# A transformer block with four mixers on one core: SBUF addresses of weight tiles, large tiles and constants, moved to 128 or 384 modulo 512

## The chip, the cores and the metric

The kernel runs on one core of one Trainium2 chip. The metric is the device time of one execution in microseconds (us). A profile of one execution was taken as well; it gives each instruction's engine, start and duration. Its engines are PE (TensorE: matmuls), PEld (TensorE's weight loads, which run beside the matmuls), DVE (VectorE), ACT (ScalarE), POOL (GpSimd) and SP (which issues DMAs).

## The reference

One block on `x` (512 tokens, width 1024): a normalised projection into four mixers of width 512 each, the mixers, an output projection with residual, and a last normalisation. All data is float32.

```python
def reference(x, mem, norm_g, w_in, ..., w_mem_kv, w_out, final_norm_g):
    for l in range(DEPTH):                                    # DEPTH = 1
        h = _rmsnorm(x, norm_g[l])
        p_fox, p_ssm, p_nsa, p_mem = _split(h @ w_in[l], [FOX_COLS, SSM_COLS, NSA_COLS, MEM_COLS])
        mem_kv = _rmsnorm(mem, mem_norm_g[l]) @ w_mem_kv[l]
        o = jnp.concatenate([
            _fox_mixer(p_fox, fox_f_bias[l]),                 # causal attention with forget gates
            _ssd_mixer(p_ssm, ...),                           # convolution and chunked state space scan
            _nsa_mixer(p_nsa, ..., rel_bias_table),           # compressed, selected and window attention
            _mem_mixer(p_mem, mem_kv),                        # attention to 256 memory tokens
        ], axis=-1)
        x = x + o @ w_out[l]
    return _rmsnorm(x, final_norm_g)
```

## The kernel before

**Number format.** Every large float32 product is done as three float32r matmuls (`three`, line 716): each operand is split into a high part and a low part, and high·high, high·low and low·high are summed in one PSUM bank. A matmul has a stationary operand of 128 x 128, loaded by a weight load (LDWEIGHTS) of its own, and a moving operand of up to 512 columns that streams past it.

**Weights.** All weights come as 75 tiles of 128 x 1024 in the order of `ORDER`. `load` brings a tile into a ring of three `raw` tiles; `split` makes its high part `wh` on ACT and its low part `wl = raw - wh` on POOL or DVE, in rings of three each (`ring`, line 568). The last eight tiles (output projection of the fourth mixer, `wo3`) are an exception: `split` puts their halves into tiles of 512 columns of the large pool `g`, by the names `lh` and `ll` (lines 605 to 609).

**Projections.** `tile_a` (line 873; PSUM tile `pj`) makes one 128 x 512 tile of a projection with 24 matmuls: stationary is a 128-column slice of `wh` or `wl`, moving are the parts `hh` and `hl` of the normalised input (512 columns, pool `g`). `proj_b` (line 762; `pb`), `mem_v` (line 1845; `pmv`) and the output projections `out_proj` and `out_last` (lines 1056 and 1086; `po`) have it the other way round: stationary is a 128-column slice of an activation (`uh`, `ul`; `mh`, `ml`; `oh`, `ol`), moving are 512 columns of `wh` or `wl` (in `out_last`, of `lh` or `ll`).

**Order.** The tile framework schedules nothing. The program's order is that of the code, with the steps of the mixers and of the projections interleaved by the written-out list `PLAN`. Each engine runs its instructions in that order and waits on semaphores.

**Where tiles lie.** Pool `g` has 58 places of 2048 bytes per partition (tiles of 512 float32 columns or less), pool `b` 12 places of 4096 bytes or a little more (`B4`, line 541), pool `sb` all rings and constants (`C1`, line 546), one after the other in the order in which the code asks for them. So a place's address follows from the sizes before it. By the tile allocation of the built program, the start addresses within a partition are, modulo 512:

| tiles | before | after |
|---|---|---|
| pool `g`, all 58 places (`hh`, `hl`, `uh`, `ul`, `oh`, `ol`, `lh`, `ll`, `mh` and the rest) | 128 | 128 |
| ring `raw` (3) | 128 | 384 |
| rings `wh`, `wl` (3 + 3) | 0 | 384 |
| pool `b`, 12 places (`xn`, `mt`, `ml`, `M`, `Rl`, `kh`, `kl`, `bt`, `acc` and the rest) | 128, 128, 256, 256, 256, 384, 0, 0, 0, 128, 256, 256 | 128, 128, 384, 384, 384, 128, 384, 384, 384, 128, 384, 384 |
| constants `ones`, `nv`, `w2`, `vcm`, `umask` | 256, 384, 384, 384, 128 | 128 each |
| constants `cst`, `x0` | 128, 128 | 384, 128 |

A 128-column slice of float32 is 512 bytes, so every stationary slice of a tile starts at the tile's own residue; so do the 512-column halves. The narrow projection `("bc", 0..2)` has slices of 296 columns (1184 bytes), which start at 0, 160 and 320 from the tile's start modulo 512.

Of the kernel before, what the change touches and what calls it, by code (L numbers as in the profile page):

```python
# [10 lines left out]
FT = mybir.dt.float32  # L11
# [19 lines left out]
RAW, RING = 3, 3  # L31
# [484 lines left out]
        return 0 < self.at[0] and self.at[-1] < len(self.steps)  # L516


@with_exitstack
def block_kernel(ctx, tc, I, out, lives):  # L520
    nc = tc.nc
# [1 line left out]
    V, A, P, T, Q = (Engine(e, n, clock, lives) for e, n in (  # L523
        (nc.vector, "DVE"), (nc.scalar, "ACT"), (nc.gpsimd, "POOL"), (nc.tensor, "PE"), (nc.sync, "SP")))
    NG, NB = 58, 12
    gp, bp, sp_, sb = (ctx.enter_context(tc.tile_pool(name=n, bufs=1)) for n in ("g", "b", "s", "sb"))
    ps = ctx.enter_context(tc.tile_pool(name="ps", bufs=1, space=bass.MemoryType.PSUM))
    dr = ctx.enter_context(tc.tile_pool(name="dr", bufs=1, space=bass.MemoryType.DRAM))
    ctx.enter_context(tc.manual_schedule())
# [2 lines left out]
    gslots, bslots = Slots("g", NG, lives, clock), Slots("b4", NB, lives, clock)  # L532
# [3 lines left out]
    def G(name, dt=FT, w=512, p=128):  # L536
        gs.take()
        tag, n = gslots.take()
        return gslots.hold(gp.tile([p, w], dt, name=name, tag=tag, bufs=n))

    def B4(name, shape, dt=FT):
        bs.take()
        tag, n = bslots.take()
        return bslots.hold(bp.tile(shape, dt, name=name, tag=tag, bufs=n))

    def C1(name, shape, dt=FT):
        n = math.prod(shape[1:])
        t = sb.tile([shape[0], -(-n // 32) * 32], dt, name=name)[:, :n]
        return t if len(shape) == 2 else t.rearrange("p (a b) -> p a b", a=shape[1])

    def SM(name, w):
        tag, n = sslots.take()
        return sslots.hold(sp_.tile([128, 64], FT, name=name, tag=tag, bufs=n))[:, :w]
# [5 lines left out]
    def PS(name):  # L559
        tag, n = pslots.take()  # L560
        t = pslots.hold(ps.tile([128, 512], FT, name=name, tag=tag, bufs=n))
        clock.bank(t.name)
        return t

    raw, wh, wl, state = {}, {}, {}, {"load": 0, "split": 0, "next": 0}
    rings = {"raw": [RAW, []], "wh": [RING, []], "wl": [RING, []]}

    def ring(name, dt):
        left = rings[name]
        t = sb.tile([128, 1024], dt, name=name, bufs={"raw": RAW, "wh": RING, "wl": RING}[name])  # L570
        assert left[0] > 0, "ring is full"
        left[0] -= 1
        if left[1]:
            clock.born[t.name] = left[1].pop(0)
        return t
# [7 lines left out]
    def load(n, wait=True):  # L583
        while state["load"] < min(n, len(ORDER)):
            i = state["load"]
            free = rings["raw"][1]
            if not wait and free and free[0] + SLACK > clock.t["PE"]:
                return
            raw[i] = ring("raw", FT)
            if i < 2:  # L590
                for h in range(2):
                    (A if i == h == 0 else Q).dma_start(out=raw[i][:, h * 512:(h + 1) * 512],
                                                        in_=I["wst"][i, :, h * 512:(h + 1) * 512])
                    if i == h == 0:
                        A.dma_start(out=x0[:, 264:520], in_=I["x0"][:, 264:520])
            else:
                Q.dma_start(out=raw[i], in_=I["wst"][i])
            state["load"] += 1

    def split(n):  # L600
        while state["split"] < min(n, len(ORDER)):
            i = state["split"]
            load(i + 1)
            halves = slice(0, 512), slice(512, 1024)
            if ORDER[i][0] == f"wo{LAST}":
                hi, lo = [G("lh", FR) for _ in halves], [G("ll", FR) for _ in halves]
                for x, h in enumerate(halves):
                    A.activation(hi[x], raw[i][:, h], AF.Copy)
                    tt(WIDE, out=lo[x], in0=raw[i][:, h], in1=hi[x].bitcast(FT), op=OP.subtract)
            else:  # L610
                hi, lo = ring("wh", FR), ring("wl", FR)
                for x, h in enumerate(halves if i < 2 else (slice(0, 1024),)):
                    if i == x == 0:
                        V.tensor_copy(out=hi[:, h], in_=raw[i][:, h])
                        low()
                    else:
                        A.activation(hi[:, h], raw[i][:, h], AF.Copy)
                    if i == x == 0:
                        V.tensor_tensor(out=lo[:, h], in0=raw[i][:, h], in1=hi.bitcast(FT)[:, h], op=OP.subtract)
                    else:  # L620
                        tt(WIDE, out=lo[:, h], in0=raw[i][:, h], in1=hi.bitcast(FT)[:, h], op=OP.subtract)
            wh[i], wl[i] = hi, lo
            unring("raw", raw.pop(i))
            state["split"] += 1
# [26 lines left out]
    def ahead():  # L651
        n = state["next"]
        load(min(n + 4, state["split"] + RAW), False)
        while can_split():
            split(state["split"] + 1)
            load(min(n + 4, state["split"] + RAW), False)

    x0 = C1("x0", [128, 632])
    vec = x0[:, 512:632]
    Q.dma_start(out=x0[:, 0:264], in_=I["x0"][:, 0:264])  # L660
    xt = [x0[:, 8:520]] + [G(f"xt{k}") for k in range(1, KT)]
    load(1)
    for k in range(1, KT):
        Q.dma_start(out=xt[k], in_=I["xT"][:, k, :])
        if k in (2, 5):
            load({2: 2, 5: 3}[k])
    xn = [B4("xn", [128, D]) for t in range(4)]
    for t in range(4):
        Q.dma_start(out=xn[t], in_=I["xn"][t])
    cst = C1("cst", [128, 788])  # L670
    Q.dma_start(out=cst, in_=I["cst"])
    Q.dma_start(out=x0[:, 520:632], in_=I["x0"][:, 520:632])
    ident, U, cmask, ind = cst[:, 0:128], cst[:, 128:256], cst[:, 256:768], cst[:, 768:776]
# [4 lines left out]
    v_pe = vec[:, 64:96]  # L678
    v_fd, v_al = vec[:, 96:112], vec[:, 112:120]

    ones = C1("ones", [128, 128])
    V.memset(ones, 1.0)
    nhalf = C1("nhalf", [128, 8])
    V.memset(nhalf, -0.5)

    seen = {}
# [41 lines left out]
    s4f = G("s4")  # L728
    P.memset(s4f, 0.0)
    fv = [G(f"fv{t}") for t in range(4)]  # L730
    nv = C1("nv", [128, 4, 296])
    uh, ul, hh, hl = [], [], [], []

    def parts(k):
# [9 lines left out]
    for k in range(KT):  # L744
# [4 lines left out]
            low()  # L749
        if k in (0, 3):  # L750
            split(1 if k == 0 else 2)
    rx = C1("rx", [128, 4])

    ss = SM("ss", 4)

# [65 lines left out]
    for i in range(2):  # L821
        t = B4("mt", [128, D])
        Q.dma_start(out=t.rearrange("p (k m) -> p k m", k=4), in_=I["memT"][:, 4 * i:4 * i + 4, :])
        mt += [t[:, 0:512], t[:, 512:1024]]
    mn = [B4("mn", [128, D]) for _ in range(2)]
    for t in range(2):
        Q.dma_start(out=mn[t], in_=I["mn"][t])
# [287 lines left out]
        "wo3": lambda k: out_last(k[1]) if LAST == 3 else out_proj(3, k[1]),  # L1115
    }

    sp = C1("sp", [128, 4, 16])
    dA = C1("dA", [128, 32])
    gat = C1("gat", [128, 4, 24])  # L1120

    crs = []

# [196 lines left out]
    rvs = B4("rvs", [8, RVW])  # L1320
    Q.dma_start(out=rvs[:, 0:512], in_=I["rel"])
    V.memset(rvs[:, 512:RVW], BIG)
    w2 = C1("w2", [128, 2, 64])
    Q.dma_start(out=w2, in_=I["w2"])
    w1 = []

# [38 lines left out]

    def win(t, n, first=0):
        return bass.AP(tensor=t.tensor, offset=t.offset + 384 - 128 * first, ap=[t.ap[0], [-128, n - first], [1, 128]])
    vcm = C1("vcm", [96, 128])

    xst = {}  # L1370

# [230 lines left out]
        gs.drop()  # L1602
        xs[i] = y

    cwh = C1("cwh", [128, 32])
    V.tensor_scalar(out=cwh, in0=v_cw, scalar1=0.5, scalar2=None, op0=OP.mult)
    cbh = C1("cbh", [128, 8])
    V.tensor_scalar(out=cbh, in0=v_cb, scalar1=0.5, scalar2=None, op0=OP.mult)
    umask = C1("umask", [128, 128])
    V.tensor_scalar(out=umask, in0=U, scalar1=BIG, scalar2=-BIG, op0=OP.mult, op1=OP.add)  # L1610


    def ssm_pre():
        pa = PS("pa")
        T.matmul(pa[:, 0:32], U, dA, start=True, stop=True)
        T.matmul(pa[:, 32:64], ones, dA, start=True, stop=True)
        nacs, dte, decR = (C1(n, [128, 32]) for n in ("nacs", "dte", "decR"))
        V.tensor_scalar(out=nacs, in0=pa[:, 0:32], scalar1=-1.0, scalar2=None, op0=OP.mult)
        V.tensor_tensor(out=dte, in0=pa[:, 32:64], in1=nacs, op=OP.add)
        A.activation(dte, dte, AF.Exp)  # L1620
        A.activation(decR, pa[:, 32:64], AF.Exp)
        dA2 = SM("dA2", 64)
        V.tensor_copy(out=dA2[:, 0:32], in_=dA)
        V.tensor_copy(out=dA2[:, 32:64], in_=dA)
        pre.extend((nacs, dte, decR))
        return dA2
# [19 lines left out]
    def prep():  # L1646
        kept = []

        def s0(_):
            kept.append(ssm_pre())  # L1650

        def s1(_):
            ssm_rows(kept.pop())
            bg.done.add("pre")

        return Pipe([0], [s0, s1], 1, [1, 1], [(0, 0), (1, 1)], 0)
# [454 lines left out]
def build(nc, arrays, lives=None):  # L2111
    lives = lives or Lives(lifetimes(arrays))
    I = {n: nc.dram_tensor("in_" + n, v.shape, mybir.dt.from_np(v.dtype), kind="ExternalInput").ap()
         for n, v in arrays.items()}
    out = nc.dram_tensor("out_0", (4, 128, 1024), FT, kind="ExternalOutput").ap()
    with tile.TileContext(nc) as tc:
        block_kernel(tc, I, out, lives)
        if lives.known is None:
            raise Rehearsed
# [11 lines left out]
```

## Time and profile before

| | |
|---|---|
| time, median of 3 runs | 517.52 us (517.48 to 517.83) |
| the profiled execution: its own time | 517.46 us |
| its span (first to last instruction) | 515.7 us |
| granted TensorE clock, mean | 0.999 |
| busy: PE, PEld, DVE, ACT, POOL | 506.8, 421.1, 357.9, 302.1, 186.4 us |
| matmul instructions | 2973 |
| DMA | 90.56 MB, mean 176 GB/s |

The profile gives busy times and counts for groups of equal instructions, the idle time before them with what ended it, and a chain of work: from the last instruction back, at each step to what released it. Matmuls are pipelined: the duration of one (some 390 ns at 512 columns) covers its way through the array, and the next one starts before it ends. What a matmul costs is the distance from its start to the next one's start, which the chain and the timeline give. In the views, `pj<-hh,wh` names the operands without regard to which is stationary, and buffer numbers are left out. Nearly all instructions stand under line 357, the helper through which every engine's call goes.

### The profile page before, as it was taken

The numbers are of one execution on the slowest core, as the hardware profiler recorded it, in microseconds if no ns is written. First come the engines' busy times: TensorE is split into PE (matmuls) and PEld (weight loads), VectorE is DVE, ScalarE is ACT, GpSimd is POOL, SyncE is SP. The second block draws the span as 40 slices with busy tenths as digits, with TensorE's granted clock in tenths as the row PEclk, the third lists the DMA queues.
The fourth block names the chain that finished last, engine by engine and source line by source line (L and its number), as shares of the span: only waits on it lengthen the run. The fifth ranks groups of instructions, "written<-read, shape, count | busy, mean of one in ns | idle before, by whom it ended". The sixth has DMA issues, their size and how long they took to land.

```text
span 515.7 us, 9000 instructions
## 1 busy us (share of the span) xinstructions
PE 506.8 (98%) x2973; PEld 421.1 (82%) x2973; DVE 357.9 (69%) x965; ACT 302.1 (59%) x680; POOL 186.4 (36%) x127
## 2 busy tenths in 40 slices
PE   8999999999999999999999999999999999999995
PEld 5898788888888888887888888887888888888884
DVE  5386687586677678897866786677777668466544
ACT  5855556665875655563456768446577755574333
POOL 2594210141231112385546452601313235117432
PEclk9999999999999999999999999999999999999999
DMA  8791832757456867533218577778865786632213
GB/s 299 308 324 51 78 126 87 243 137 229 126 145 199 253 182 249 179 126 121 92 60 291 146 191 226 217 225 238 246 179 140 231 233 204 195 119 82 83 41 122
DMA packets 71246, 90.56 MB, mean 176 GB/s; under 512 B 26640, under 2 KB 50448, under 8 KB 71200
## 3 DMA queue, kind: packets, MB, share of 16 engines
q1 hardware_dynamic: 70768, 89.40, 57.2%
q10 hardware_dynamic: 432, 0.59, 0.3%
q8 instruction: 23, 0.38, 0.3%
q14 instruction: 23, 0.19, 0.1%
HBM read 71.59 MB, written 20.53 MB: 179 GB/s over the span
## 4 chain that ended last, share of the span: by engine, by line
PE 92%; DVE 3%; ACT 2%; issue 2%; POOLq 0%; POOL 0%; DVEq 0%; ACTq 0%
PE pj L357 47%; PE po L357 16%; PE pb L357 7%; PE pO L357 7%; PE pS L357 5%; PE pmv L357 2%; PE pW L357 1%; PE pT L357 1%; PE pY L357 1%; DVE pN L357 1%; PE pcm L357 1%; PE pw L357 1%; DVE yc L357 1%; ACT pN L357 1%; ACT m L357 0%
## 5 line engine op out<-in xcount | busy, mean ns | idle before, releaser
L357 POOL TENSOR_TENSOR wl<-raw,wh 128x1024 fp32r<-128x1024 f32 (+1 forms) x53 | 127.6, 2412 | 247.8 <-ACT wh L357 235.1
L357 PE MATMUL pj<-hh,wh 128*128 128x512 f32 x352 | 141.4, 402 | 0.0
L357 PE MATMUL pj<-hh,wl 128*128 128x512 f32 x352 | 138.9, 395 | 0.0
L357 PE MATMUL pj<-hl,wh 128*128 128x512 f32 x352 | 138.8, 394 | 0.0
L357 ACT ACTIVATE wh<-raw 128x1024 fp32r<-128x1024 f32 (+1 forms) x72 | 74.3, 1034 | 9.2 <-PE po L357 3.2
L357 PEld LDWEIGHTS pj<-hh,wl 128*128 128x128 f32 x352 | 66.2, 188 | 15.7
L357 PEld LDWEIGHTS pj<-hh,wh 128*128 128x128 f32 x352 | 66.3, 188 | 14.9 <-issue 1.0
L357 PEld LDWEIGHTS pj<-hl,wh 128*128 128x128 f32 x352 | 66.3, 188 | 13.4
L357 ACT ACTIVATE pN<-pN,nm 128x128 f32<-128x128 f32 (+7 forms) x96 | 45.5, 474 | 34.3 <-DVE nm L357 33.0
L357 PE MATMUL po<-wh,oh 128*128 128x512 f32 x96 | 38.8, 404 | 0.0
L357 PE MATMUL po<-wh,ol 128*128 128x512 f32 x96 | 38.0, 396 | 0.0
L357 PE MATMUL po<-wl,oh 128*128 128x512 f32 x96 | 37.8, 394 | 0.0
L357 DVE STREAM_TRANSPOSE fl<-pN 128x128 f32<-128x128 f32 (+3 forms) x64 | 28.5, 485 | 0.1
L357 DVE TENSOR_TENSOR acc<-acc,po 128x512 f32<-128x512 f32 (+1 forms) x33 | 21.0, 662 | 10.5 <-PE po L357 10.4
L357 ACT ACTIVATE pF<-pF,nm 128x128 f32<-128x128 f32 (+3 forms) x32 | 17.8, 556 | 17.2 <-DVE nm L357 15.0
L357 DVE TENSOR_TENSOR wl<-raw,wh 128x1024 fp32r<-128x1024 f32 (+1 forms) x20 | 23.4, 1168 | 5.8 <-ACT wh L357 5.6
L357 DVE SCALAR_TENSOR_TENSOR rs<-sm,gat 128x3 f32<-128x3 f32 x32 | 6.6, 207 | 28.0 <-ACT pN L357 28.0
L357 DVE CUSTOM_DVE_ANT_0 pN<-pS,bt 128x128 f32<-128x128 f32 (+5 forms) x80 | 22.4, 319 | 3.2 <-PE pS L357 2.1
L357 ACT ACTIVATE pN<-pN,rs 128x512 f32<-128x512 f32 (+3 forms) x28 | 15.9, 594 | 11.4 <-DVE rs L357 11.4
L357 DVE SCALAR_TENSOR_TENSOR xs<-x,cwh,xs 128x512 f32<-128x512 f32 x24 | 18.0, 750 | 5.8 <-ACT xs L357 5.1
L357 PEld LDWEIGHTS po<-wh,ol 128*128 128x128 f32 x96 | 18.1, 188 | 4.5 <-DVE ol L357 0.3
L357 PEld LDWEIGHTS po<-wh,oh 128*128 128x128 f32 x96 | 18.1, 188 | 3.6 <-PE pY L357 0.2
(280 smaller groups left out, 1027.4 us busy)
## 6 DMA issues: line engine op xcount, KB each, us to landing
raw<-in_wst SPq DMA_DIRECT2D x73, 512.0 KB, 4.1
far<-fl SPq DMA_DIRECT2D x144, 64.0 KB, 1.8
pt<-far SPq DMA_DIRECT2D x36, 256.0 KB, 3.6
far<-fl SPq DMA_DIRECT2D x96, 48.0 KB, 2.8
pt<-far SPq DMA_DIRECT2D x24, 192.0 KB, 3.9
rows<-rv SPq DMA_DIRECT2D x4, 656.0 KB, 8.0
bt<-rows SPq DMA_DIRECT2D x4, 528.0 KB, 4.9
xn<-in_xn SPq DMA_DIRECT2D x4, 512.0 KB, 7.5
```

Source lines behind the costliest of these rows:

```text
L357: return f(*a, **k)
```

## The change

Only addresses change. On all five engines the instructions stand in the same order, with the same shapes and the same semaphore waits as before, so no row of the program's order moves.

- The `raw`, `wh` and `wl` rings get a pool of their own (`rp`). A constant of 256 bytes (`sp`) lies ahead of it in another (`tp`), so that the rings start at 384 modulo 512.
- `B4` goes through a new helper `wide`, which pads a tile to a multiple of 64 columns (256 bytes). Of the tiles in pool `b` those of 1056 columns (`kh`, `kl`, `bt`) become 1088 columns, the one of 656 (`rvs`) 704.
- The constants come from a list `CONSTS`, in its order, ahead of all other tiles, padded to 8 columns (32 bytes) in place of 32 columns; `C1(name)` then only takes one from the list.

```diff
+CONSTS = {"ones": [128, 128], "umask": [128, 128], "vcm": [96, 128], "w2": [128, 2, 64], "sp": [128, 4, 16],
+          "nv": [128, 4, 296], "dA": [128, 32], "cst": [128, 788], "nhalf": [128, 8], "cbh": [128, 8], "rx": [128, 4],
+          "pad": [128, 16], "x0": [128, 632], "gat": [128, 4, 24], "cwh": [128, 32], "nacs": [128, 32],
+          "dte": [128, 32], "decR": [128, 32]}
...
-    gp, bp, sp_, sb = (ctx.enter_context(tc.tile_pool(name=n, bufs=1)) for n in ("g", "b", "s", "sb"))
+    gp, bp, tp, rp, sp_, sb = (ctx.enter_context(tc.tile_pool(name=n, bufs=1)) for n in ("g", "b", "t", "r", "s", "sb"))
...
     def B4(name, shape, dt=FT):
         bs.take()
         tag, n = bslots.take()
-        return bslots.hold(bp.tile(shape, dt, name=name, tag=tag, bufs=n))
-
-    def C1(name, shape, dt=FT):
+        t, view = wide(bp, name, shape, dt, tag=tag, bufs=n)
+        bslots.hold(t)
+        return view
+
+    def wide(pool, name, shape, dt, unit=64, **kw):
         n = math.prod(shape[1:])
-        t = sb.tile([shape[0], -(-n // 32) * 32], dt, name=name)[:, :n]
-        return t if len(shape) == 2 else t.rearrange("p (a b) -> p a b", a=shape[1])
+        t = pool.tile([shape[0], -(-n // unit) * unit], dt, name=name, **kw)
+        v = t[:, :n]
+        return t, v if len(shape) == 2 else v.rearrange("p (a b) -> p a b", a=shape[1])
+
+    fixed = {n: wide(tp if n == "sp" else sb, n, shape, FT, 8)[1] for n, shape in CONSTS.items()}
+
+    def C1(name):
+        return fixed.pop(name)
...
-        t = sb.tile([128, 1024], dt, name=name, bufs={"raw": RAW, "wh": RING, "wl": RING}[name])
+        t = rp.tile([128, 1024], dt, name=name, bufs={"raw": RAW, "wh": RING, "wl": RING}[name])
...
-    x0 = C1("x0", [128, 632])
+    x0 = C1("x0")
...
```

The other lines of the diff only drop the shape from a call of `C1`, as for `x0`.

More of the change, by code (lines that the diff above doesn't have):

```diff
@@ L669, in block_kernel @@
         Q.dma_start(out=xn[t], in_=I["xn"][t])
-    cst = C1("cst", [128, 788])
+    cst = C1("cst")
     Q.dma_start(out=cst, in_=I["cst"])
@@ L679, in block_kernel @@
     v_fd, v_al = vec[:, 96:112], vec[:, 112:120]
-    ones = C1("ones", [128, 128])
+    ones = C1("ones")
     V.memset(ones, 1.0)
-    nhalf = C1("nhalf", [128, 8])
+    nhalf = C1("nhalf")
     V.memset(nhalf, -0.5)
@@ L730, in block_kernel @@
     fv = [G(f"fv{t}") for t in range(4)]
-    nv = C1("nv", [128, 4, 296])
+    nv = C1("nv")
     uh, ul, hh, hl = [], [], [], []
@@ L751, in block_kernel @@
             split(1 if k == 0 else 2)
-    rx = C1("rx", [128, 4])
+    rx = C1("rx")
     ss = SM("ss", 4)
@@ L1116, in block_kernel @@
     }
-    sp = C1("sp", [128, 4, 16])
-    dA = C1("dA", [128, 32])
-    gat = C1("gat", [128, 4, 24])
+    sp = C1("sp")
+    dA = C1("dA")
+    gat = C1("gat")
     crs = []
@@ L1322, in block_kernel @@
     V.memset(rvs[:, 512:RVW], BIG)
-    w2 = C1("w2", [128, 2, 64])
+    w2 = C1("w2")
     Q.dma_start(out=w2, in_=I["w2"])
@@ L1367, in win @@
         return bass.AP(tensor=t.tensor, offset=t.offset + 384 - 128 * first, ap=[t.ap[0], [-128, n - first], [1, 128]])
-    vcm = C1("vcm", [96, 128])
+    vcm = C1("vcm")
     xst = {}
@@ L1603, in s_conv @@
         xs[i] = y
-    cwh = C1("cwh", [128, 32])
+    cwh = C1("cwh")
     V.tensor_scalar(out=cwh, in0=v_cw, scalar1=0.5, scalar2=None, op0=OP.mult)
-    cbh = C1("cbh", [128, 8])
+    cbh = C1("cbh")
     V.tensor_scalar(out=cbh, in0=v_cb, scalar1=0.5, scalar2=None, op0=OP.mult)
-    umask = C1("umask", [128, 128])
+    umask = C1("umask")
     V.tensor_scalar(out=umask, in0=U, scalar1=BIG, scalar2=-BIG, op0=OP.mult, op1=OP.add)
@@ L1616, in ssm_pre @@
         T.matmul(pa[:, 32:64], ones, dA, start=True, stop=True)
-        nacs, dte, decR = (C1(n, [128, 32]) for n in ("nacs", "dte", "decR"))
+        nacs, dte, decR = (C1(n) for n in ("nacs", "dte", "decR"))
         V.tensor_scalar(out=nacs, in0=pa[:, 0:32], scalar1=-1.0, scalar2=None, op0=OP.mult)
```

## The prediction

> **What bounds the kernel now.** First the page: busy times, granted clock, and the chain that ended last.
>
> ```profile
> span 515.7 us, 9000 instructions
> PE 506.8 (98%) x2973; PEld 421.1 (82%) x2973; DVE 357.9 (69%) x965; ACT 302.1 (59%) x680; POOL 186.4 (36%) x127
> ...
> PEclk9999999999999999999999999999999999999999
> ...
> PE 92%; DVE 3%; ACT 2%; issue 2%; POOLq 0%; POOL 0%; DVEq 0%; ACTq 0%
> PE pj L357 47%; PE po L357 16%; PE pb L357 7%; PE pO L357 7%; PE pS L357 5%; PE pmv L357 2%; PE pW L357 1%; PE pT L357 1%; PE pY L357 1%; DVE pN L357 1%; PE pcm L357 1%; PE pw L357 1%; DVE yc L357 1%; ACT pN L357 1%; ACT m L357 0%
> ```
>
> TensorE is busy throughout at full clock, and 92% of the chain is TensorE; pj, po, pb and pmv, the 512-column matmuls on weight tiles, make 72% of the span. The profiled execution took 517.46 us, its span is 515.7, and 1.8 us lie around it; it stands 0.06 us under the median of 517.52. Next, who makes TensorE wait: the longest rows of the waits of PE and of its weight loads.
>
> ```profile
> PE pw L357 <- DVE warm L357: 1.3, 1, 1.3
> PE pT L357 <- DVE pcp L357: 0.8, 1, 0.8
> PE pn L357 <- DVE sq L357: 0.5, 1, 0.5
> ```
> ```profile
> PEld pO L357 <- issue: 3.4, 11, 0.4
> PEld L357 <- issue: 1.7, 6, 0.3
> ```
>
> Hardly anything does: 2.6 us in all for PE, single waits under 1.4 us. So a nanosecond off each matmul is a nanosecond off the end, as long as the others keep up. The question is then what the distance between two matmuls depends on. The groups of matmuls by form give the first hint (busy time, mean duration in ns of one):
>
> ```profile
> L357 PE MATMUL pj<-hh,wl 128*128 128x512 f32 x352 | 138.9, 395 | 0.0
> ...
> L357 PE MATMUL po<-wl,oh 128*128 128x512 f32 x96 | 37.8, 394 | 0.0
> ...
> L357 PE MATMUL po<-lh,ol 128*128 128x512 f32 x28 | 10.9, 390 | 0.0
> L357 PE MATMUL po<-ll,oh 128*128 128x512 f32 x28 | 10.9, 390 | 0.0
> L357 PE MATMUL po<-lh,oh 128*128 128x512 f32 x28 | 10.9, 389 | 0.0
> ...
> L357 PE MATMUL pb<-wl,uh 128*128 128x512 f32 x32 | 8.8, 395 | 0.0
> ...
> L357 PE MATMUL pmv<-wl,mh 128*128 128x512 f32 x16 | 6.3, 395 | 0.0
> ```
>
> The po matmuls on `lh` and `ll` are of the same form as those on `wh` and `wl`, and 4 to 6 ns shorter. The chain in order of time (start, length, instructions) shows this as distance from start to start:
>
> ```profile
> 316.43 10.46 PE pj L357 x45
> ...
> 387.72 7.69 PE pj L357 x33
> ...
> 464.21 10.46 PE po L357 x45
> ...
> 486.75 19.79 PE po L357 x87
> ```
>
> 10.46 / 45 = 232.4 ns, 7.69 / 33 = 233.0, again 232.4, but 19.79 / 87 = 227.5 in the last stretch, the one on `lh` and `ll`. What differs there? Not the load on the chip, by the busy times of these stretches (us, then PE, PEld, DVE, ACT, POOL with counts, clock, DMA share, GB/s):
>
> ```profile
> 316.43:326.89 10.46, 10.46 (x47) 8.21 (x48) 8.46 (x21) 5.90 (x13) 7.00 (x4) 1.00 0.77 250
> ...
> 464.21:474.67 10.46, 10.46 (x47) 8.43 (x47) 6.73 (x10) 5.38 (x11) 7.42 (x5) 1.00 0.15 51
> 489.00:506.00 17.00, 17.00 (x77) 14.06 (x76) 7.36 (x15) 5.98 (x15) 5.94 (x5) 1.00 0.16 62
> ```
>
> At a DMA share of 0.77 and of 0.15 the distance is 232.4 alike; the last row has the second one's DMA and a similar mix of engines, at the same clock. What is left is the addresses. In the last stretch stationary (`oh`, `ol`) and moving (`lh`, `ll`) both lie at 128 modulo 512; elsewhere one of them is `wh` or `wl` at 0 and the other at 128. The timeline shows the change at the very step (start, length):
>
> ```profile
> 487.28 0.40 PE L357 MATMUL po<-lh,oh 128*128 128x512 f32 x1
> ...
> 489.36 0.39 PE L357 MATMUL po<-lh,oh 128*128 128x512 f32 x1
> ...
> 506.14 0.39 PE L357 MATMUL po<-lh,ol 128*128 128x512 f32 x1
> 506.36 0.28 PE L357 MATMUL po<-lh,oh 128*128 128x256 f32 x1
> ...
> 506.96 0.28 PE L357 MATMUL po<-lh,ol 128*128 128x256 f32 x1
> ```
>
> The first nine distances on `lh`, `ll` are 2.08 / 9 = 231 ns, the 74 after them 16.78 / 74 = 226.8, and single ones there are 226 or 227 without exception, where the other stretches swing between 228 and 241. At 256 columns in the same tiles it is 0.60 / 5 = 120. So **two operands in step give a steady 226.8; 128 bytes out of step they give about 232.5**.
>
> **The change part by part.** It puts `wh`, `wl` at 384, against 128 for `hh`, `hl`, `uh`, `ul`, `oh`, `ol`, `mh`: 256 apart, not in step modulo 512. Is 256 as good as 0? The memory projection answers: its moving `wh` lies at 0, `mh` at 128, and its `ml` at 0 for the first four k and at 256 for the last four.
>
> ```profile
> 271.42 0.40 PE L357 MATMUL pmv<-wh,ml 128*128 128x512 f32 x1
> ...
> 273.52 0.40 PE L357 MATMUL pmv<-wh,ml 128*128 128x512 f32 x1
> ...
> 277.27 0.39 PE L357 MATMUL pmv<-wh,ml 128*128 128x512 f32 x1
> ...
> 279.37 0.40 PE L357 MATMUL pmv<-wh,ml 128*128 128x512 f32 x1
> ```
>
> From 271.42 to 273.52 `ml` is at 0, from 277.27 to 279.37 at 256; both are three rounds of three matmuls in 2.10 us, and inside a round the distances are the same 233, 232, 235. A shift by 256 is not seen, so I take the period as 256 and the new layout as in step. (One operand in three in step helps nothing: 2.10 / 9 = 233.3. All must be, and after the change they are.)
>
> *The main term.* By the counts above, 3 x (352 + 96 + 32 + 16) = 1488 matmuls of 512 columns have a `wh` or `wl` operand. Followed through the timeline, 1361 of their distances are undisturbed (two 512-column matmuls in direct succession, under 262 ns), with a mean of 232.5; the others begin or end a stretch. If each falls to 226.8: 1361 x 5.7 = **7.8 us**. If each of the 83 unbroken stretches spends nine distances at the old rate, as the last one did, 799 are left: 799 x 5.7 = **4.6 us**. I take the middle, 6.2, since one observed start says little about the others. Of this the share that is on TensorE's part of the chain reaches the end: 6.2 x 0.92 = **5.7 us**.
>
> *The narrow projection (96 matmuls of 296 columns).* Its slices start 160 bytes apart, so padding can't put them in step.
>
> ```profile
> 30.08 0.70 PE L357 MATMUL pb<-wh,uh 128*128 128x296 f32 x4
> 30.62 0.71 PE L357 MATMUL pb<-wh,ul 128*128 128x296 f32 x4
> ```
> ```profile
> 36.10 0.72 PE L357 MATMUL pb<-wh,uh 128*128 128x296 f32 x4
> 36.66 0.72 PE L357 MATMUL pb<-wh,ul 128*128 128x296 f32 x4
> ```
>
> With the moving operand at 160 four take 0.54 us (135 each), at 320 they take 0.56 (140). The worst and the best offset differ by 5 ns, 96 x 5 = 0.5 us either way; I take 0. The matmuls of 128 to 416 columns in the mixers are fewer and already have mostly pool `g` operands; 0, with the same 0.5 us as bound.
>
> *The other engines.* `raw` and `wh` come into step too (128 and 0 before, 384 both after), which two-operand work on POOL and DVE might feel.
>
> ```profile
> L357 POOL TENSOR_TENSOR wl<-raw,wh 128x1024 fp32r<-128x1024 f32 x51 | 124.5, 2446 | 239.4 <-ACT wh L357 226.8 <-DMA far<-fl 5.9 <-DVE sums L357 3.6
> ...
> L357 POOL TENSOR_TENSOR ll<-raw,lh 128x512 fp32r<-128x512 f32 x6 | 8.6, 1461 | 2.0 <-ACT lh L357 2.0
> ```
>
> `ll<-raw,lh` has both operands at 128, in step: 2 x 1461 = 2922 ns for 1024 columns, against 2446. Since that doubles the fixed part too, it is an upper bound: 476 ns more on each of 51, and nothing the lower. POOL idles 239 us ahead of these very instructions, and `wl` is made a tile ahead, 24 x 232 = 5.6 us; so 0 on the path. DMAs only land elsewhere; no wait is added or removed.
>
> Sum: 517.46 - 5.7 = **511.8 us**.
>
> **The skill's view.** The Trainium skill, "TensorE: Matmul & The Clock Gate", section "Step-by-step: what each phase is for", says that TensorE reads stationary and moving operands through two independent ports, and that "Loading the next tile's weights doesn't steal SBUF read bandwidth from the running matmul"; "SBUF — State Buffer", section "Who interferes with whom", has PE waiting for no one. By that the layout is worth nothing and the time stays at 517.5. The trace disagrees where it can be tested: 226.8 against 232.4 ns for one form. The first page's "Back-to-back issue gap" gives 512 / 2.4 + 2.5, an estimate of 215.8 ns for a lone matmul; no distance here settles there.
>
> **Rivals.**
> - *No effect.* The last stretch is steady for a reason other than addresses, or steadiness needs 0 modulo 512. Against it: equal traffic, equal form, the change at 487.28 to 489.36, and the pmv rounds. For it: one stretch alone shows the low rate, and pmv is a mixture. 517.5 us.
> - *Slower: 256 apart is its own bad case in pj.* A distance can depend on the offset in both directions (135 against 140 at 296 columns, 3.7%). If a steady pattern at 256 is as slow as the slow half of today's swing, about 238 ns, it costs 1361 x 5.5 = 7.5 us: 525. It decides once the mean passes 232.5. Against it: the pmv rounds with `ml` at 256.
> - *Given back.* TensorE gains 4.6 us or less and runs into DVE and ACT, which are 8% of the chain already; half is lost: 515.
> - *Much better.* 256 apart has no interference at all. 226.8 at 512 columns and 120 at 256 make 106.8 / 256 = 0.417 ns a column, so 213.6 for 512 with 13.2 on top; without these 1361 x 18.9 = 26 us less: 492. Nothing in the rows hints at it.
>
> That the new addresses aren't as stated is excluded: both allocations are known.
>
> **How the numbers follow.** In step: 0.62 (509.0 to 514). Given back: 0.13. No effect: 0.13. Slower: 0.09. Much better: 0.03. A measurement of this kernel can tell about 0.2%, 1 us, from no change: faster 0.62 + 0.13 + 0.03 = 0.78, same 0.13, slower 0.09. Range: 509.0 (7.8 us and 0.5 of the narrow ones) to 517.6, which takes in "given back" and half of "no effect"; left out are the rest of that, "slower" and "much better", some 0.19.
>
> **What would show it.** Right: mean durations of the pj and po groups fall from 394 and 395 to about 390, pieces of the chain on pj come to 227 to 229 ns a matmul with single distances of 226 and 227, the stretch on `lh`, `ll` stays at 227.5, and DVE and ACT keep their share of the chain. Wrong: pj and po durations unchanged, or a new steady distance above 232.5; or the distances fall and waits of PE on DVE, ACT or `wl` appear, which is "given back".

## The result

The changed kernel takes 514.24 us (median of four runs, 513.93 to 514.35) against 517.67 us for the kernel before in the same comparison (517.48 to 518.21): a ratio of 0.9931, 95% interval 0.9914 to 0.9948. A second comparison gave 514.66 against 518.43 us, ratio 0.9923 (0.9909 to 0.9936). Faster was predicted, at 511.8 us; the time lies inside the range of 509.0 to 517.6, 2.4 us above the forecast and 0.2 above the 509.0 to 514 given there for the case "in step".

The profiled execution took 514.34 us. Its page first: span, busy times, clock and the chain that ended last.

```profile
span 512.5 us, 9000 instructions
...
PE 501.6 (98%) x2973; PEld 420.8 (82%) x2973; DVE 357.0 (70%) x965; ACT 302.1 (59%) x680; POOL 186.4 (36%) x127
...
PEclk9999999999999999999999999999999999999999
...
PE 49%; DVE 15%; DMA 12%; ACT 12%; issue 6%; POOL 4%; SPq 2%; POOLq 0%; DVEq 0%; ACTq 0%
```

TensorE is busy for 5.2 us less (506.8 before), the span is 3.2 us shorter, and the chain has changed its nature: 49% on PE instead of 92%. A chain that leaves PE does not yet say that PE waits long, only that somewhere it waited and that what it waited for is followed back from there. First the matmuls by form (busy us, mean ns of one, idle time and what ended it):

```profile
L357 PE MATMUL pj<-hh,wl 128*128 128x512 f32 x352 | 137.4, 390 | 0.3 <-DVE wl L357 0.3
...
L357 PE MATMUL po<-wl,oh 128*128 128x512 f32 x96 | 37.5, 391 | 0.0
...
L357 PE MATMUL po<-lh,oh 128*128 128x512 f32 x28 | 10.9, 389 | 0.0
```

pj fell from 395 to 390 ns and po from 394 to 391, to what the matmuls on `lh` and `ll` had already (389, unchanged). The pieces of the chain give the distance from start to start:

```profile
314.69 10.24 PE pj L357 x45
...
385.38 7.51 PE pj L357 x33
...
461.39 10.23 PE po L357 x45
...
483.62 19.76 PE po L357 x87
```

10.24 / 45 = 227.6 ns, 7.51 / 33 = 227.6, 227.3, and 227.1 for the last stretch, which was at 227.5. Where such matmuls follow one another without a break, here called a stretch, the timeline of PE shows how the steady distance is reached:

```profile
314.76 0.39 PE L357 MATMUL pj<-hl,wh 128*128 128x512 f32 x1
...
316.84 0.39 PE L357 MATMUL pj<-hl,wh 128*128 128x512 f32 x1
...
324.55 0.39 PE L357 MATMUL pj<-hh,wl 128*128 128x512 f32 x1
```

Nine distances in 2.08 us are 231 ns each; the 34 after them, in 7.71 us, 226.8. Over all stretches the mean distance by position is 232.0, 233.0, 231.1, 229.1, 230.2, 229.4, 227.8, 228.2 and 227.8 ns for the first nine and 226.5 to 226.8 from the tenth to the thirtieth; before it was 231 to 234 at every position. The mean over all 1443 undisturbed distances between 512-column matmuls on weight tiles fell from 232.2 to 228.1 ns (the stretch on `lh`, `ll` included), which is 1443 x 4.1 = 5.9 us.

So PE got what was expected of it. Where is the rest? Both traces run the same matmuls in the same order, so the distances can be compared one by one. All those that changed by less than 60 ns sum to 6.38 us gained. Twelve places changed by more, the other way: 3.39 us lost, of which 0.58 stand at 66 us, 1.71 around 211 us and 0.50 at 298 us; one place won 0.17. That leaves 3.16 us. The longest of these places are seen in the waits of PE:

```profile
PE pcm L357 <- DMA w<-in_w: 1.3, 1, 1.3
PE pT L357 <- DVE pcp L357: 1.0, 2, 0.6
...
PE pj L357 <- DVE wl L357: 0.3, 1, 0.3
```

**At 211 us** `pcm`, the compression step of the third mixer, needs the loads `w1` (four tiles `w<-in_w` of 512 KB, `load_w1`). The timeline of PE before and after, and that of SP (which issues the loads) after and before:

```profile
212.87 3.71 PE L357 MATMUL pcm<-w,xp 128*64 128x128 f32 x64
```
```profile
209.89 0.43 PE L357 MATMUL pcm<-w,xp 128*64 128x128 f32 x2
211.65 3.68 PE L357 MATMUL pcm<-w,xp 128*64 128x128 f32 x62 [1.33 <-DMA w<-in_w]
```
```profile
196.71 5.46 SPq L357 DMA_DIRECT2D raw<-in_wst  x2
202.21 1.86 SPq L357 DMA_DIRECT2D w<-in_w  x4
```
```profile
197.75 5.46 SPq L357 DMA_DIRECT2D raw<-in_wst  x2
203.25 1.93 SPq L357 DMA_DIRECT2D w<-in_w  x4
```

PE comes to `pcm` 2.98 us earlier than before, the loads are issued only 1.04 us earlier. Ahead of them in SP's queue stand two raw loads, on which SP spends 5.46 us; 4.8 of these it waits for `wl` on DVE to free the second one's place in the ring.

**At 66 us** a chain of a load, ACT and DVE ends in `wl`:

```profile
52.20 11.73 DMA raw<-in_wst
...
64.01 1.07 ACT wh L357
...
65.10 1.23 DVE wl L357
...
66.38 0.73 PE pj L357 x2
```

A raw load of 512 KB, a size that takes 3.1 us to land at 202 us and 4.1 in the median of the whole trace, lands 11.7 us after its issue. In SP's queue it stands right behind `rmd`, 1 KB written in rows of 4 bytes, which is itself issued only at 51.70, once its data are there: SP waits 11.0 us for them, and the loads behind `rmd` with it. **At 298 us** a transposition waits for `pcp` on DVE, which ends only 1.15 us earlier than in the kernel before, while PE gets there 2.1 us earlier.

### The profile page after: what moved, and what is told of

It is laid out like the page before. It is cut to its first block, busy times and chain, and to the rows that moved or that the text cites. A ratio compares the mean times of both kernels' runs of the same rounds, so it can differ in the third digit from the quotient of the medians.

```text
span 512.5 us, 9000 instructions
## 1 busy us (share of the span) xinstructions
PE 501.6 (98%) x2973; PEld 420.8 (82%) x2973; DVE 357.0 (70%) x965; ACT 302.1 (59%) x680; POOL 186.4 (36%) x127
## 4 chain that ended last, share of the span: by engine, by line
PE 49%; DVE 15%; DMA 12%; ACT 12%; issue 6%; POOL 4%; SPq 2%; POOLq 0%; DVEq 0%; ACTq 0%
PE pj L357 22%; PE po L357 14%; PE pO L357 5%; DMA raw<-in_wst 4%; ACT pF L357 4%; PE pS L357 3%; DVE fl L357 3%; POOL wl L357 3%; ACT pN L357 2%; DMA far<-fl 2%; DMA xt<-in_xT 2%; DVE xs L357 2%; SPq L357 2%; ACT wh L357 2%; DMA w<-in_w 2%
## 5 line engine op out<-in xcount | busy, mean ns | idle before, releaser
L357 PE MATMUL pj<-hh,wl 128*128 128x512 f32 x352 | 137.4, 390 | 0.3 <-DVE wl L357 0.3
L357 PE MATMUL pj<-hl,wh 128*128 128x512 f32 x352 | 137.4, 390 | 0.0
L357 ACT ACTIVATE th<-xs 128x512 f32<-128x512 f32 x8 | 5.1, 632 | 26.9 <-DVE xs L357 26.9
```

The source lines that it names most:

```text
L357: return f(*a, **k)
```

## The experiments

**Theory:** two operands whose addresses are equal modulo 256 run in step, which means that the distance settles near 227 ns; the rings alone bring that about; much of what PE gains is handed back at loads whose arrival a faster PE does not move. **Rivals:** the padded blocks or the list of constants do it; only 384 is good, or any address that keeps away from 0 and 128; a faster PE simply meets DVE and ACT, wherever the loads stand.

### Where the rings lie

Four kernels differ from the changed one only in which constants lie ahead of the rings (pool `tp`) and which behind (a new pool `up`, opened after `rp`); the blocks keep the new addresses. As the edit for rings at 0:

```diff
-    gp, bp, tp, rp, sp_, sb = (ctx.enter_context(tc.tile_pool(name=n, bufs=1)) for n in ("g", "b", "t", "r", "s", "sb"))
+    gp, bp, tp, rp, up, sp_, sb = (ctx.enter_context(tc.tile_pool(name=n, bufs=1)) for n in ("g", "b", "t", "r", "u", "s", "sb"))
...
-    fixed = {n: wide(tp if n == "sp" else sb, n, shape, FT, 8)[1] for n, shape in CONSTS.items()}
+    fixed = {n: wide(tp if n in ('sp', 'nacs') else up if n in ('gat',) else sb, n, shape, FT, 8)[1] for n, shape in CONSTS.items()}
```

For 128 nothing lies ahead and `sp` behind; for 192 `nhalf`, `cbh` ahead and `nacs`, `pad` behind; for 160 `nhalf` ahead and `nacs`, `pad`, `cbh` behind; in these two `sp` also goes to the end of the list of constants. In all but the first some small constants shift as well.

> The changed kernel, with raw, wh and wl at 128 modulo 512 in place of 384: in step with pool g modulo 512, 256 away from the change. Theory (period 256): nothing changes against the changed kernel: single distances of 226 and 227 ns, mean duration of pj<-hh,wl 390, time 514.2 within 1 us. Rival (256 of 512 apart is what helps, period 512): mean distance 230 or more, 516 to 518 us, or, if 0 is even better than 256, under 513.

> The changed kernel, with raw, wh and wl back at 0 modulo 512; blocks and constants as in the change. Theory (the rings alone make the gain): distances of 228 to 241 ns again with a mean of 232.5, pj<-hh,wl 394 to 395, time 517.5 within 0.7 us. Rival (blocks and constants make it): 514.2.

> The changed kernel, with raw, wh and wl at 192 modulo 512, 64 out of step with pool g. Theory (every offset but 0 modulo 256 disturbs; the 296-column row at such an offset took 140 against 135 ns): no steady 227, mean distance 232 to 240, time 517 to 525. Rival (only an offset of 128 is bad): 227 and 514.

> The changed kernel, with raw, wh and wl at 160 modulo 512, 32 out of step with pool g. Theory (step must be exact): mean distance 230 or more, 516 to 520 us. Rival (some play is allowed, as lines or banks of some size would give): 227 and 514.

Measured (the moving or stationary operand in pool `g` lies at 128 throughout; the distances are means over 1443 pairs or a few less):

| rings at | out of step modulo 256 | time, us | ratio to before (95%) | mean distance, ns | pj with wl, ns |
|---|---|---|---|---|---|
| 128 | 0 | 514.89 | 0.9925 (0.99 to 0.9951) | 228.1 | 390 |
| 384 (the change) | 0 | 514.24 | 0.9931 (0.9914 to 0.9948) | 228.1 | 390 |
| 0 | 128 | 517.96 | 0.9991 (0.9982 to 1.0001) | 232.0 | 395 |
| 192 | 64 | 517.83, one run | | 232.2 | 395 |
| 160 | 32 | 518.71, one run | | 232.8 | 396 |

The first, third and last kernels' groups of the one form, each from its own list of groups:

```profile
L357 PE MATMUL pj<-hh,wl 128*128 128x512 f32 x352 | 137.4, 390 | 0.5 <-DVE wl L357 0.5
```
```profile
L357 PE MATMUL pj<-hh,wl 128*128 128x512 f32 x352 | 139.0, 395 | 0.0
```
```profile
L357 PE MATMUL pj<-hh,wl 128*128 128x512 f32 x352 | 139.3, 396 | 0.0
```

128 and 384 are alike, so if the pattern repeats at all, its period is 256 or a divisor of it, and since 128, 64 and 32 bytes apart are not in step, it is 256 itself. Out of step by 128, 64 or 32 bytes the mean is back at 232 to 233 ns, and no stretch of 15 distances or more has a mean under 228.5 from its tenth on, where in the changed kernel every such stretch has 226.6 to 226.8. Out of step they do repeat patterns, only others: at 160, for example, distances of 231 or 232 and 235 in turn. So it isn't enough to keep away from 0 and 128: equality counts. At 192 the mean hides a difference: pj, where the weights are stationary, has 233.4 ns, but po, pb and pmv, where the weights move, have 230.7, 229.2 and 229.5 (232.4, 233.1 and 232.9 in the kernel before). That is one run, and no kernel put the rings 64 bytes away on the other side, so what the sign of the offset does stays open. So does whether equal addresses other than 128 and 384 do as well, since pool `g` was never moved and no stretch had all its operands at another equal pair. With the rings back at 0 the new blocks and constants are worth nothing that can be measured. The other way round, the kernel before with only the rings moved to 384:

```diff
-    gp, bp, sp_, sb = (ctx.enter_context(tc.tile_pool(name=n, bufs=1)) for n in ("g", "b", "s", "sb"))
+    gp, bp, rp, sp_, sb = (ctx.enter_context(tc.tile_pool(name=n, bufs=1)) for n in ("g", "b", "r", "s", "sb"))
...
-        t = sb.tile([128, 1024], dt, name=name, bufs={"raw": RAW, "wh": RING, "wl": RING}[name])
+        t = rp.tile([128, 1024], dt, name=name, bufs={"raw": RAW, "wh": RING, "wl": RING}[name])
```

> The kernel before with one thing changed: the wh, wl and raw rings moved to a pool of their own at 384 modulo 512; blocks and constants keep their addresses of before. Theory (the rings alone carry the gain): 514.2 us within 0.5, pj groups at 390 to 391 ns for the two with hl or wl, mean distance near 228.1 ns. Rival (the padded blocks and the list of constants carry a part, for example through steady pT, pS and pY matmuls): half of the gain or less, 515.5 to 517.5 us.

514.34 us, ratio 0.9915 (0.9902 to 0.9928), pj at 391 and 390 ns, mean distance 228.1: within the noise these two lines carry the whole gain. The trace shows one place that still needs the moved blocks, the memory projection: here `ml` stays at 0 and 256, 128 bytes out of step with the rings at 384, and its two longest stretches average 231.2 ns each, against 228.4 and 227.5 in the changed kernel (some 0.2 us in all). So rings at 384 are not good by themselves, only together with an operand in step.

### Where the gain goes: the loads of w1

First the order of the four loads, for in the code all halves of `j = 0` come before those of `j = 1`, while the second matmul of `pcm` wants `j = 1` already:

```diff
-        for j in range(2):
-            w1.append([B4("w1", [128, 8, 128]) for _ in range(2)])
-            for h in range(2):
+        for j in range(2):
+            w1.append([B4("w1", [128, 8, 128]) for _ in range(2)])
+        for h in range(2):
+            for j in range(2):
                 Q.dma_start(out=w1[j][h], in_=I["w1"][j, :, h * 8:(h + 1) * 8, :])
```

> The changed kernel with the four w1 loads issued in the order in which pcm uses them (both halves 0 first, then both halves 1); the tiles keep their places. Theory (1.3 to 1.6 us of the PE gain are given back at pcm because the third load issued is needed by the second matmul): the wait of pcm on DMA falls from 1.3 us to between 0 and 0.7, and the time falls by as much, to 512.9 to 513.5 us. Rival (what is gained there is waited for again further on, on DVE, ACT or the weight halves): the wait goes and the time stays at 514.2.

> The same order of the four w1 loads in the kernel before. Both theories: no wait of pcm on DMA there to take away, so 517.5 us within 0.5; a gain here would mean that the order of the loads is worth something by itself and that the other run cannot be read as a gain handed back.

In the changed kernel 514.48 us, ratio 0.9918 (0.9904 to 0.9932); in the kernel before 518.45 us, 0.9999 (0.999 to 1.0008). Against the change's 0.9931 and 0.9923 nothing can be told apart. The timeline shows a miss:

```profile
210.73 2.18 PE L357 MATMUL pcm<-w,xp 128*64 128x128 f32 x34
213.69 1.93 PE L357 MATMUL pcm<-w,xp 128*64 128x128 f32 x30 [0.78 <-DMA w<-in_w]
```

In the trace the wait moved from ahead of the third matmul to ahead of the 35th and shrank from 1.33 to 0.78 us, and nothing of that is seen in the time. `pcm` now waits for the last of the four, so the arrival of all four matters more than their order. The next kernels therefore moved the loads themselves, and the small `rmd` as well. The raw loads of tiles 35 and 36 go behind `w1` (`late`), and `rmd` goes behind the raw loads of tiles 11 and 12 (`rms`); the first and the second kernel have one of the two edits, the others both:

```diff
-                Q.dma_start(out=raw[i], in_=I["wst"][i])
+                if i in (35, 36):
+                    late.append((raw[i], i))
+                else:
+                    Q.dma_start(out=raw[i], in_=I["wst"][i])
+            if i == 12:
+                Q.dma_start(out=rmd.rearrange("t p -> p t"), in_=rms[0])
...
                 Q.dma_start(out=w1[j][h], in_=I["w1"][j, :, h * 8:(h + 1) * 8, :])
+        for t, i in late:
+            Q.dma_start(out=t, in_=I["wst"][i])
...
-        Q.dma_start(out=rmd.rearrange("t p -> p t"), in_=r)
+        rms.append(r)
```

> The changed kernel with the four w1 loads issued ahead of the two raw loads (tiles 35 and 36) that wait some 5.5 us for a ring place in SP's queue; the raw loads follow right behind. Theory (part of the PE gain is handed back because w1 lands at a time that a faster PE does not move): pcm has no wait on DMA, and the ratio to the kernel before falls from 0.993 to about 0.990 to 0.9915. Rivals: the places of w1 in pool b are not free any earlier, so the loads start as late as now and the wait stays; or the two raw loads come late and PE waits for their halves instead; both leave the ratio at 0.992 to 0.994.

> The changed kernel with the small DMA rmd (1 KB, in rows of 4 bytes) issued behind the raw loads of tiles 11 and 12 in SP's queue; before it stood ahead of both and they landed 10 to 12 us after issue. Theory (the wait of pj on wl near 66 us is this load handing back 0.6 to 0.9 us): the wait goes, later parts keep the lead, the ratio falls by 0.001 to 0.002, to 0.991 to 0.992. Rival: the small rows delay the next raw load instead, and the wait moves to the tile behind.

> Both moves of the two runs above in the changed kernel. Theory: the two waits go and the ratio comes to 0.989 to 0.9905 (5.2 to 5.7 us of the 6.4 us that PE gains arrive). Rival (other engines take up whatever PE gains): 0.992 to 0.994 as without.

> Both moves in the kernel before, rings at 0. Theory: the wait on w1 is not there and the wait on wl near 66 us is 0 to 0.5 us, so the ratio is 0.999 to 1.000. Rival: the moves are worth the same 1 to 2 us in the kernel before, ratio 0.996 to 0.998; then the two waits are not what the change's gain ran into but a loss that both kernels have.

> The changed kernel as it is, timed once more against the kernel before, because the runs with moved loads were compared with the kernel before on another occasion. Theory (the two waits on loads take 1.5 to 2.5 us of the gain): ratio 0.991 to 0.994, above the 0.9884 of the run with both loads moved. Rival (the changed kernel would have come to 0.9884 on that occasion as well, and the moved loads did nothing): ratio under 0.990.

| kernel | time, us | before, us | ratio (95%) |
|---|---|---|---|
| the change | 514.24 | 517.67 | 0.9931 (0.9914 to 0.9948) |
| the change, again | 514.66 | 518.43 | 0.9923 (0.9909 to 0.9936) |
| + w1 first | 513.46 | 518.27 | 0.9906 (0.9893 to 0.992) |
| + rmd later | 512.91 | 518.27 | 0.9893 (0.9879 to 0.9908) |
| + both | **512.43** | 518.27 | **0.9884** (0.9871 to 0.9898) |
| kernel before + both | 517.68 | 518.27 | 0.9991 (0.9982 to 1.0) |

Two of these ratios lie under what was expected: `rmd` later alone came to 0.9893 in place of 0.991 to 0.992, though its trace still has 1.0 us of the wait of `pcm`, and both moves to 0.9884 in place of 0.989 to 0.9905. The single moves add up to more than both together, by less than their intervals allow to tell. The change and both moves together are worth 5.84 us, with an interval clear of those of the change alone. In the kernel before the same moves bring 0.59 us, with an interval that reaches from 0 to 0.93: there PE mostly came late enough for the loads (though not always: the profiled execution of the kernel before with the other order of `w1` waits 0.7 us at 67 and 68 us, for the same raw load). By the ratios they bring 2.0 to 2.4 us in the changed kernel, so most of that is gain of the new addresses that had been lost at these loads. Waits of PE, `pcm` and SP's queue in the kernel with both:

```profile
PE pT L357 <- DVE pcp L357: 1.6, 2, 0.9
PE pw L357 <- DVE warm L357: 1.3, 1, 1.3
PE pn L357 <- DVE sq L357: 0.5, 1, 0.5
PE pb L357 <- ACT uh L357: 0.3, 1, 0.3
```
```profile
209.69 3.71 PE L357 MATMUL pcm<-w,xp 128*64 128x128 f32 x64
```
```profile
196.63 2.15 SPq L357 DMA_DIRECT2D w<-in_w  x4
198.96 5.71 SPq L357 DMA_DIRECT2D raw<-in_wst  x3
```

The loads start at 196.63 instead of 202.21, `pcm` runs through, and neither `w` nor `wl` is in the list. PE makes up 89% of the chain again. The move of `rmd` does two things: the first of the two raw loads is issued at 43.20 us in place of 52.20, since it no longer waits for the data of `rmd`, and the second lands 3.2 us after its issue in place of 12.5. The delay moves on to the next raw load, as the rival had it: issued at 57.78, now behind `rmd`, it takes 6.8 us; but PE has no wait there. By distances, this kernel's trace against that of the kernel before with both moves has 6.5 us gained and 2.1 lost, 0.84 of it at `pcp` and 0.28 still at 66 us. The wait for `pcp` stands at 1.6 us, against 1.0 in the changed kernel. It is 0.7 or 0.8 in the six traces with rings out of step and 0.9 to 1.6 in the eight with rings in step, so it comes with the faster PE; that it grows with PE's lead is not shown, since the changed kernel has 1.0 in one execution and 1.5 in another.

The run of the change again scatters (513.51 to 516.14 us) more than the kernel with both (512.12 to 512.75), and its trace shows one cause. The profiled execution is its slowest, 516.14 us:

```profile
66.70 0.50 PE L357 MATMUL pj<-hh,wh 128*128 128x512 f32 x1 [1.04 <-ACT wh L357]
...
67.96 0.50 PE L357 MATMUL pj<-hh,wl 128*128 128x512 f32 x1 [0.53 <-DVE wl L357]
```

Here the raw load behind `rmd` landed later still, 13.2 us after its issue, and the place at 66 us took 2.1 us in place of 0.58 (distances of 1429, 337, 923 and 337 ns instead of 241, 233, 237 and 232). How long the load behind `rmd` takes varies from execution to execution (11.7 and 13.2 us here); why was not tried.

## Why the prediction was right, and where it was off

- *In step at 256 apart:* right. The rows of the memory projection only hinted at it, since they settle at neither offset; rings at 128 and at 384, with the same 228.1 ns, show it.
- *The steady distance and the start of a stretch:* right. 226.8 ns was taken, 226.5 to 226.8 came; nine distances at the old rate were taken from one stretch, and the mean over all stretches settles at the tenth, though the fourth to the ninth lie already at 227.8 to 230.2.
- *The size on PE:* right. 6.2 us were taken (the middle of 7.8 and 4.6; no row chose the middle, so that it came this near is partly luck). The undisturbed 512-column distances gave 5.9, all small changes together 6.38. Nearly all of the difference too stands behind 512-column matmuls on weight tiles, where a matmul of another form follows: 6.32 of the 6.38 us are distances that begin at one.
- *The narrow projection and other engines:* right at 0. Four matmuls of 296 columns still take 0.53 to 0.55 us, and all 96 together gained 0.14; `wl` on POOL 2444 ns against 2446, although its two operands came into step too.
- *The share that reaches the end:* the mis-sized term. The prediction multiplied 6.2 by 0.92, PE's share of the chain, and got 5.7. The profiled execution kept 3.16 of 6.38, a half. The share of a chain says where PE was the last to be ready; it says nothing of how soon the next one would be late. The question to each engine and queue was not "how often is it on the chain" but "by how much did it beat PE", and at two loads that was less than the 1 to 3 us by which PE would be ahead there. "As long as the others keep up" stood in the text, and was followed up for POOL, not for SP's queue and the loads behind it. Taken apart by the runs: with the two loads out of the way 5.25 us arrive against the kernel before with the same moves (517.68 - 512.43), and 5.84 against the kernel before without them.
- *Signs:* one sign of being right failed, and one of being wrong came. DVE and ACT did not keep their share of the chain (3% and 2% before, 15% and 12% after), and a wait of pj on `wl` appeared, which the prediction had named as "given back". The range held because it was drawn wide enough for that rival. Its lower end, 509.0, lies 0.2 us under its own sum (517.46 - 7.8 - 0.5); nothing hung on that.
- *Rival "given back":* it named DVE and ACT, a gain of 4.6 us or less, and 515 us. The time is nearest to it, and half of the gain was lost as it says, but PE had gained 6.38. The mechanism was another: mostly DMA, by the loads of `w1` and the one behind `rmd`; DVE took a smaller part at `pcp`. That last part was only read from traces, since no run moved that step.
- *No effect, slower, much better:* excluded, by the steady 226.7 ns at two ring addresses and by 232 to 233 at three others.

The prediction weighed a rule of the Trainium skill, "TensorE: Matmul & The Clock Gate", section "Step-by-step: what each phase is for", by which loading the next weights doesn't steal read bandwidth from the running matmul. It took from it that the layout is worth nothing, and the measurement decides against that for this kernel. The same instructions in the same order differ by 4 ns in 232, with the rings moved and nothing else (ratio 0.9915). That it is the weight loads' reads that cost the time is not shown: only the start addresses were varied.

## What to carry to other kernels

Where a kernel is bound, as this one, by float32r matmuls with a weight load each, look at start-to-start distances in long stretches: if they swing in one stretch and are steady in another of the same form, compare the operands' start addresses modulo 256 and put the rings of weights where the activations are. A gain on the bounding engine should be charged, before it is promised, with the slack of every load and engine that it waits for (arrival against need, in us), not with the chain's share. And a load that stands in a queue behind a small DMA or behind one that waits for a buffer arrives at a time of its own, which a faster engine moved little here (1.04 us of 2.98 at `w1`).

## What the runs showed of the hardware

- Float32r matmuls with a 128 x 128 weight load each settle at 226.7 ns for 512 columns when stationary and moving operand start at equal addresses modulo 256, after about nine of them; 32, 64 or 128 bytes apart they don't come down to that and average 232.8, 232.2 and 232.0. In step, each started at 128 or 384 modulo 512; no stretch had all its operands at another equal pair.
- `wl = raw - wh` on POOL or DVE does not feel this: 2446 and 1221 ns per tile out of step, 2444 and 1220 in step.
- A DMA of 1 KB in rows of 4 bytes holds up what is queued behind it. With `rmd` ahead, the next load of 512 KB landed 11.7 us after issue; with `rmd` behind the two loads, the second of them landed in 3.2 us (the landing of the first is not in the trace), `rmd` itself took 9.7, and the load behind `rmd`, issued 6 us after it, took 6.8.

By the DMA issues of the kernel with both moves between 42 and 56 us (issuer, count, size of each, median us to landing of those whose landing was traced):

```profile
raw<-in_wst SPq DMA_DIRECT2D x2, 512.0 KB, 3.2
rmd<-rmr SPq DMA_DIRECT2D x1, 1.0 KB, 9.7
```
